# Two-layer hybrid trunk on one core: modulation sums given to other engines, weights' low parts last in a first tile, and GQA's and MLA's transpositions one tile later

## The chip, the cores and the metric

The kernel runs on one core of a Trainium2 chip. The metric is the time of one execution in device microseconds: 1836.56 us before the change, the median of 3 runs (1835.67 to 1840.74).

## The reference: what is computed

Two layers of a hybrid trunk for 9 token tiles of 128 (one of context, eight of latent tokens), model width 1024. Each layer makes a modulation from a condition (two rows: context and latent), normalises, shifts and scales, and then does one wide input projection whose columns go to four head groups:

```python
shift, scale, gate = jnp.split(silu(c) @ w_ada[l] + b_ada[l], 3, axis=-1)
h = rms_norm(x, p['norm_pre']) * (1 + scale) + shift
u = h @ p['w_in']
qa = rms_norm(gq.reshape(B, N, GQA_HEADS, HEAD_DIM), p['gqa_q_norm'])   # GQA: rotated, then attention
cq = rms_norm(mcq, p['mla_q_norm']); ckv = rms_norm(mckv, p['mla_kv_norm'])   # MLA
xbc = jax.nn.silu(centred_dwconv(sxbc, p['ssd_conv_w'], p['ssd_conv_b']))   # SSD
...
o = jnp.concatenate([o_a, o_b, o_c, o_d], axis=-1) @ p['w_out']
y = x + gate * rms_norm(o, p['norm_post'])
```

The change lies in the input projection `h @ w_in` and in the modulation of layer 1, which is computed beside the input projection of layer 0.

## The kernel before

The input projection of a layer is done in pieces of columns, one after the other: LV (512 columns, with GLA's values), SM (296 small columns), MG (gates of MLA), XBC (the columns that SSD's convolution takes), GQA (512), MLA (352), and UQ and QK (MLA's second projection and GLA's q and k). This is called a stage here. Attention, the scans and the output projection follow.

*Products.* Weights and activations are split into a high and a low part, and three products are made per block k of 128 rows (8 blocks): whi·hh, whi·hl and wlo·hh, 24 matmuls per tile. `load_w` brings one block: SP issues the DMA of wst (2 buffers in layer 0, 4 in layer 1), DVE casts it to whi (L257), POOL subtracts to get wlo (L261). `proj_tok` puts tokens on the partitions, and has one PSUM tile per token tile; `proj_T` puts columns on the partitions, and has one PSUM tile of 384 tokens for each of three chunks of every 128 columns (6 in MG, 12 in XBC and in QK). Four PSUM tiles psP go round (`psAB`). A tile is handed to `consume`, which empties it: in GQA (`cons_gqa`) ACT squares it (sq), DVE sums per head (ss, L606), POOL takes the power -0.5 (L107), DVE scales from PSUM (z, L609), POOL and DVE rotate (L611 to L626, r), TensorE transposes r three times (gT, L629) and ACT copies the result. `cons_mla` does the like, with transposes mT (L677).

*Order in a tile before.* `proj_tok` takes, in its first two tiles, all whi·hh and wlo·hh by k and then the eight whi·hl; in the others, and always in `proj_T`, the three products of one k together.

*Modulation.* `ada_steps` is a generator that makes half a part of a modulation (part 1 scale, part 0 shift, part 2 gate; half 0 and 1) in nine steps: for each k it loads 256 KB (ast, 2 buffers) and adds ast times the condition's two rows (r = 0 and 1) into acc; then TensorE sums acc over partitions (ada, L183 for part 2, L189 for the others). For k = 0 ACT writes acc. Else a row's sum is one DVE instruction (L176), or, for r = 1 of part 2, a product on ACT (pr, L173) and a sum on POOL (L174):

```python
elif r and part == 2:
    act.activation(out=pr, in_=st, func=AF.Identity, scale=c)
    pool.tensor_tensor(out=acc[:, r, :], in0=acc[:, r, :], in1=pr, op=ALU.add)
else:
    dve.scalar_tensor_tensor(out=acc[:, r, :], in0=st, scalar=c, ...)
```

`steps_` holds the generators that run in layer 0's projections: part 2 of layer 0 and the six halves of layer 1. `proj_tok` takes two steps after an even tile and one after an odd one, `proj_T` one after each tile.

*What sets the order.* The program is built with a scheduler that simulates it and places each instruction on its engine when it is ready; the program's text only gives the priority. On the chip each engine works through its list in that order, so a waiting instruction holds all behind it on its engine.

Of the kernel before, what the change touches and what calls it, by code (L numbers as in the profile page):

```python
# [12 lines left out]
ALU = mybir.AluOpType  # L13
# [6 lines left out]
KD = 8  # L20
# [14 lines left out]
def hybrid_trunk_kernel(ctx: ExitStack, tc: tile.TileContext, a):  # L35
# [14 lines left out]
    def psC(name="psC"):  # L50
        return ps.tile([128, 512], F32, name=name, tag="C", bufs=1)
# [107 lines left out]
    def ada_steps(l, parts, wpool, ac, sc, d_gate):  # L159

        for part, half in parts:
            o = part * D + half * 512
            acc = wpool.tile([128, 2, 512], F32, name="acc", tag="acc", bufs=1)
            for k in range(KD):
                st = wpool.tile([128, 512], F32, name="ast", tag="ast", bufs=2)
                sp.dma_start(out=st, in_=a["w_ada"][l, k * 128:(k + 1) * 128, o:o + 512])
                for r in range(2):
                    c = cc[:, k, r:r + 1]
                    if k == 0:
                        act.activation(out=acc[:, r, :], in_=st, func=AF.Identity, scale=c)  # L170
                    elif r and part == 2:
                        pr = wpool.tile([128, 512], F32, name="pr", tag="pr", bufs=1)
                        act.activation(out=pr, in_=st, func=AF.Identity, scale=c)  # L173
                        pool.tensor_tensor(out=acc[:, r, :], in0=acc[:, r, :], in1=pr, op=ALU.add)  # L174
                    else:
                        dve.scalar_tensor_tensor(out=acc[:, r, :], in0=st, scalar=c, in1=acc[:, r, :], op0=ALU.mult, op1=ALU.add)  # L176
                yield
            p = psC("ada")
            if part == 2:
# [88 lines left out]

    def proj_tok(l, hh, hl, wpool, off, n, consume, rows=iter(())):
        ws = [load_w(a["w_in"][l, k * 128:(k + 1) * 128, off:off + n], n, wpool) for k in range(KD)]  # L270
        next(rows, None)
        next(rows, None)
        for t in range(T):
            next(rows, None)
            p = psAB()
            s = slice(t * 128, (t + 1) * 128)
            pairs = [(k, x, i) for k in range(KD) for x, i in ((hh, 0), (hh, 1), (hl, 0))]
            if t < 2:
                pairs.sort(key=lambda z: z[1] is hl)
            pairs = [(x[:, k, s], ws[k][i][:, 0:n]) for k, x, i in pairs]  # L280
            mm3(p[:, 0:n], pairs)
            consume(t, p)
            for _ in range(2 - t % 2):
                next(steps_[0], None)

    def proj_T(l, hh, hl, wpool, off, nct, consume, after=None):
        n = nct * 128
        ws = [load_w(a["w_in"][l, k * 128:(k + 1) * 128, off:off + n], n, wpool) for k in range(KD)]
        for ct in range(nct):
            c = slice(ct * 128, (ct + 1) * 128)  # L290
            for ch in range(3):
                s = slice(ch * 384, (ch + 1) * 384)
                p = psAB()
                pairs = []
                for k in range(KD):
                    hi, lo = ws[k]
                    pairs += [(hi[:, c], hh[:, k, s]), (hi[:, c], hl[:, k, s]), (lo[:, c], hh[:, k, s])]
                mm3(p[:, 0:384], pairs)
                consume(ct, ch, p)
                next(steps_[0], None)  # L300
            if after is not None:
                after(ct)
# [76 lines left out]
    for l in range(L):  # L379
# [83 lines left out]
        with st1:  # L463
# [134 lines left out]
            def cons_gqa(t, p):  # L598
# [27 lines left out]
                dve.tensor_tensor(out=r, in0=r, in1=sq, op=ALU.add)  # L626
                tp = psD("gT")
                for i in range(3):
                    pe.transpose(tp[:, i * 128:(i + 1) * 128], r[:, i * 128:(i + 1) * 128], ident)  # L629
                act.copy(qT[:, :, t * 128:(t + 1) * 128], tp[:, 0:256].rearrange("p (a b) -> p a b", b=128))  # L630
                act.copy(kT[:, kt * 128:(kt + 1) * 128], tp[:, 256:384])

            proj_tok(l, hh, hl, wp, G_GQA, 512, cons_gqa)

# [16 lines left out]
            def cons_mla(t, p):  # L651
# [23 lines left out]
                pool.tensor_tensor(out=kr, in0=kr, in1=r[:, 0:32], op=ALU.add)  # L675
                tp = psD("mT")
                pe.transpose(tp[:, 0:128], z[:, 0:128], ident)  # L677
                pe.transpose(tp[0:64, 128:256], z[:, 128:192], ident)
                pe.transpose(tp[:, 256:384], z[:, 192:320], ident)
                s = slice(t * 128, (t + 1) * 128)  # L680
                act.copy(c1h[:, s], tp[:, 0:128])
                dve.tensor_tensor(out=c1l[:, s], in0=tp[:, 0:128], in1=c1h[:, s], op=ALU.subtract)
                act.copy(c2s[0:64, s], tp[0:64, 128:256])
                dve.tensor_tensor(out=c2s[64:128, s], in0=tp[0:64, 128:256], in1=c2s[0:64, s], op=ALU.subtract)
                s = slice(kt * 128, (kt + 1) * 128)
                act.copy(ckh[:, s], tp[:, 256:384])
                dve.tensor_tensor(out=ckl[:, s], in0=tp[:, 256:384], in1=ckh[:, s], op=ALU.subtract)

# [792 lines left out]
```

## Time and profile before

| | before |
|---|---|
| median of 3 runs | 1836.56 us (1835.67 to 1840.74) |
| profiled execution | 1836.28 us, its span 1834.5 us |
| mean granted clock of TensorE | 0.973 |
| busy: PE, DVE, ACT, POOL | 1718.5, 1177.2, 859.9, 729.2 us |
| layer 0, SM to QK | 102.67 to 422.32 us |
| layer 1, SM to QK | 1014.63 to 1296.38 us |

PE is TensorE's matmul, DVE VectorE, ACT ScalarE, POOL GpSimd, SP the queue that issues most DMAs. PEclk is the clock that TensorE was granted, as a share of full speed. Idle time is given with the instruction that ended it.

### The profile page before, as it was taken

The page shows a single profiled execution, that of the slowest core. Times are in us where ns is not written, and L with a number is a line of the kernel's source. Part 1 is how long each engine was busy: PE and PEld are TensorE (multiplying, and loading weights), DVE is VectorE, ACT ScalarE, POOL GpSimd, SP SyncE. Part 2 cuts the span into 40 slices and gives each one's busy share as a digit, 9 for nine tenths or more (in the row PEclk, how much of TensorE's full clock was granted, in tenths as well). Part 3 has the DMA queues.
Part 4 walks back from the last instruction along what each step waited for, and adds up shares of the span by engine and source line. Part 5 has one row for each costly group of instructions (what it writes and reads, how often), then busy time and mean ns, then how long its engine had stood idle before and what let it go on. Part 6 is the DMA issues. An engine that isn't in the chain of part 4 may idle for free.

```text
span 1834.5 us, 25155 instructions
## 1 busy us (share of the span) xinstructions
PE 1718.5 (94%) x8200; PEld 1312.8 (72%) x8200; DVE 1177.2 (64%) x2297; ACT 859.9 (47%) x1907; POOL 729.2 (40%) x909
## 2 busy tenths in 40 slices
PE   8999998998998998999999999999999899899998
PEld 2787977896665666656887999889666666565676
DVE  5738887647877886772453447543776788678223
ACT  4634422434654765673442162132465467567322
POOL 3633149824343543330343323871434354333011
PEclk9999988999989999999999999999998999999999
DMA  8435353413323321142433333231442332114243
GB/s 296 138 117 156 113 168 103 129 63 119 115 77 85 90 79 47 41 144 86 138 129 104 102 94 91 60 102 37 122 116 76 81 88 83 50 36 149 87 137 115
DMA packets 179684, 190.99 MB, mean 104 GB/s; under 512 B 29406, under 2 KB 140720, under 8 KB 179552
## 3 DMA queue, kind: packets, MB, share of 16 engines
q1 hardware_dynamic: 174208, 179.11, 32.1%
q10 hardware_dynamic: 5344, 10.26, 1.7%
q8 instruction: 65, 1.06, 0.3%
q14 instruction: 67, 0.55, 0.1%
HBM read 141.00 MB, written 48.30 MB: 103 GB/s over the span
## 4 chain that ended last, share of the span: by engine, by line
PE 54%; DVE 17%; DMA 11%; POOL 7%; issue 5%; ACT 4%; SPq 1%; ACTq 0%; POOLq 0%; DVEq 0%
PE psP L267 19%; PE op L267 8%; PE st L1102 5%; PE po L1118 5%; DMA ast<-in_w_ada_dram 2%; PE mx L755 2%; DMA wst<-in_w_in_dram 2%; DVE mx L756 2%; DVE Pl L1110 2%; PE po L1114 1%; DVE acc L176 1%; DMA R<-d_rec 1%; POOL wlo L261 1%; DVE d_DT L1023 1%; PE go L931 1%
## 5 line engine op out<-in xcount | busy, mean ns | idle before, releaser
L756 DVE TENSOR_REDUCE mx<-mx 128x1 f32<-128x512 f32 (+2 forms) x400 | 224.6, 582 | 92.2 <-PE mx L755 90.6
L267 PE MATMUL psP<-whi,hh 128*128 128x512 f32 (+2 forms) x576 | 202.6, 363 | 6.1 <-DVE whi L257 3.7
L267 PE MATMUL psP<-wlo,hh 128*128 128x512 f32 (+2 forms) x576 | 202.8, 361 | 2.1 <-POOL wlo L261 1.9
L267 PE MATMUL psP<-whi,hl 128*128 128x512 f32 (+2 forms) x576 | 187.5, 359 | 0.1
L261 POOL TENSOR_TENSOR wlo<-wst,whi 128x512 fp32r<-128x512 f32 (+3 forms) x106 | 130.6, 1240 | 137.9 <-DVE whi L257 79.0
L267 PE MATMUL psP<-hh,whi 128*128 128x384 f32 x480 | 163.1, 340 | 4.7 <-DVE whi L257 3.8
L1102 PE MATMUL st<-QA,KA 128*128 128x512 f32 (+1 forms) x336 | 164.0, 488 | 0.6 <-DVE Pl L1110 0.4
L267 PE MATMUL psP<-hl,whi 128*128 128x384 f32 x480 | 160.2, 336 | 0.0
L267 PE MATMUL psP<-hh,wlo 128*128 128x384 f32 x480 | 155.0, 337 | 0.1
L1110 DVE TENSOR_TENSOR Pl<-st,Ph 128x512 fp32r<-128x512 f32 x160 | 109.7, 686 | 65.9 <-ACT st L1108 64.2
L1107 ACT ACTIVATE Ph<-st 128x512 fp32r<-128x512 f32 x160 | 95.5, 597 | 107.5 <-PE st L1102 99.1
L1117 ACT ACTIVATE P<-st 128x512 f32<-128x512 f32 (+1 forms) x176 | 99.8, 567 | 79.1 <-PE st L1102 67.1
L1102 PE MATMUL st<-QB,KB 66*128 66x512 f32 (+3 forms) x336 | 133.0, 401 | 0.0
L267 PEld LDWEIGHTS psP<-whi,hh 128*128 128x128 f32 x576 | 110.3, 193 | 20.3 <-DVE whi L257 5.2
L267 PEld LDWEIGHTS psP<-wlo,hh 128*128 128x128 f32 x576 | 110.4, 193 | 17.9 <-POOL wlo L261 5.3
L267 PEld LDWEIGHTS psP<-whi,hl 128*128 128x128 f32 x576 | 108.5, 192 | 12.4 <-DVE hl L226 0.3
L1102 PEld LDWEIGHTS st<-QA,KA 128*128 128x128 f32 x336 | 65.4, 195 | 49.8 <-issue 39.3
L267 PEld LDWEIGHTS psP<-hh,whi 128*128 128x128 f32 x480 | 90.1, 188 | 12.0 <-DVE whi L257 5.5
L1102 PE MATMUL st<-QB,KA 96*128 96x512 f32 (+1 forms) x168 | 93.2, 555 | 2.1 <-ACT P L1117 1.8
L1108 ACT ACTIVATE st<-st 128x512 f32<-128x512 f32 x160 | 94.8, 592 | 0.0
L1118 PE MATMUL po<-P,vm 128*65 128x512 f32 (+1 forms) x176 | 88.7, 586 | 5.9 <-ACT P L1117 3.4
L1144 POOL TENSOR_TENSOR gt<-gt,R 128x512 f32<-128x512 f32 (+1 forms) x24 | 26.6, 1106 | 166.0 <-DMA R<-d_rec 162.3
(369 smaller groups left out, 4325.2 us busy)
## 6 DMA issues: line engine op xcount, KB each, us to landing
ast<-in_w_ada_dram SPq DMA_DIRECT2D x96, 256.0 KB
wst<-in_w_in_dram SPq DMA_DIRECT2D x64, 256.0 KB
wost<-in_w_out_dram SPq DMA_DIRECT2D x16, 512.0 KB
d_xs<-d_xb SPq DMA_DIRECT2D x32, 192.0 KB
ot<-d_oT SPq DMA_DIRECT2D x18, 320.0 KB
d_tok<-vv SPq DMA_DIRECT2D x18, 256.0 KB
d_gt<-gg SPq DMA_DIRECT2D x24, 192.0 KB
g_qk<-d_qk SPq DMA_DIRECT2D x36, 128.0 KB
```

The source lines that it names most:

```text
L176: dve.scalar_tensor_tensor(out=acc[:, r, :], in0=st, scalar=c, in1=acc[:, r, :], op0=ALU.mult, op1=ALU.add)
L261: eng.tensor_tensor(out=lo[:, 0:n], in0=st[:, 0:n], in1=hi[:, 0:n], op=ALU.subtract)
L267: pe.matmul(p, lhsT=lt, rhs=rh, start=(first and i == 0), stop=(last and i == n - 1))
L755: pe.matmul(p[:, 0:n], lhsT=lt_m[:, s], rhs=rh_m[:, o:o + n], start=True, stop=True)
L756: dve.tensor_reduce(out=mx[:, t, i:i + 1], in_=p[:, 0:n], axis=AX.X, op=ALU.max)
L1102: anchors["pe"] = pe.matmul(sp_[:, 0:nq], lhsT=kx[:, ks], rhs=qx[:, qs], start=(i == 0), stop=(i == len(spasses) - 1))
L1107: act.activation(out=Ph[:, 0:nq], in_=sp_[:, 0:nq], func=AF.Exp, scale=scale)
L1108: anchors["act"] = act.activation(out=sp_[:, 0:nq], in_=sp_[:, 0:nq], func=AF.Exp, scale=scale)
L1110: anchors["dve"] = dve.tensor_tensor(out=Pl[:, 0:nq], in0=sp_[:, 0:nq], in1=Ph[:, 0:nq], op=ALU.subtract)
L1117: anchors["act"] = act.activation(out=P[:, 0:nq], in_=sp_[:, 0:nq], func=AF.Exp, scale=scale)
L1118: pe.matmul(po[0:65, 0:nq], lhsT=v[:, kt, vi, :], rhs=P[:, 0:nq], start=(j == 0), stop=last, skip_group_check=True)
L1144: pool.tensor_tensor(out=g[:, 0:nq], in0=g[:, 0:nq], in1=R[:, 0:nq], op=ALU.mult)
```

## The change

- `ada_steps`: the row r = 1 goes to ACT and POOL also for part 1 (both halves); for part 2, half 0, of layer 1 only for odd k. There is one more `yield`, ahead of the matmuls, so half a part has ten steps.
- `proj_tok` takes two steps after every tile (GQA one), `proj_T` one (MG two).
- In the first tile of `proj_tok` (LV excepted) and of `proj_T` the order is eight whi·hh, eight whi·hl, eight wlo·hh. The second tile of `proj_tok` keeps its order.
- GQA's and MLA's transposes, and the copies behind them, are returned as a function `rest`, which is called after the next tile has been consumed.

```diff
-                    elif r and part == 2:
+                    elif r and (part != 0 if part < 2 or half else k % 2 or l == 0):
...
                 yield
+            yield
             p = psC("ada")
...
-    def proj_tok(l, hh, hl, wpool, off, n, consume, rows=iter(())):
+    def proj_tok(l, hh, hl, wpool, off, n, consume, rows=iter(()), pace=2):
...
+        rest = None
         for t in range(T):
...
-            if t < 2:
+            if t == 0 and off != G_LV:
+
+                pairs.sort(key=lambda z: (z[2], z[1] is hl))
+            elif t < 2:
                 pairs.sort(key=lambda z: z[1] is hl)
...
-            consume(t, p)
-            for _ in range(2 - t % 2):
+
+            last, rest = rest, consume(t, p)
+            if last is not None:
+                last()
+            for _ in range(pace):
                 next(steps_[0], None)
...
+        if rest is not None:
+            rest()
+
+    def proj_T(l, hh, hl, wpool, off, nct, consume, after=None, pace=1):
...
+                pairs = [(i, x, k) for k in range(KD) for i, x in ((0, hh), (0, hl), (1, hh))]
+                if ct + ch == 0:
+                    pairs.sort(key=lambda z: (z[0], z[1] is hl))
...
-                next(steps_[0], None)
+                for _ in range(pace):
+                    next(steps_[0], None)
...
-            proj_T(l, hh, hl, wp, G_MG, 2, lambda ct, ch, p: gate_out(d_gt[2 + ct], ch, p))
+            proj_T(l, hh, hl, wp, G_MG, 2, lambda ct, ch, p: gate_out(d_gt[2 + ct], ch, p), pace=2)
...
+                def rest():
+                    tp = psD("gT")
...
+                return rest
+
+            proj_tok(l, hh, hl, wp, G_GQA, 512, cons_gqa, pace=1)
```

In `cons_mla` the lines from `tp = psD("mT")` to the last subtraction become a `rest` in the same way. Lines move: L176 stays, L257 becomes L258, L261 L262, L267 L268, L606 L616, L609 L619.

TensorE, end of MG's first tiles in layer 0, where the last of the eight weight blocks comes in. psP_1596 (before) and psP_1614 (after) are the first tile, the other psP the three that are open beside it; whi_1592 and whi_1610 are the last block's high part. Before:

```order
L183 MATMUL ada_1730<-acc_1347,pick_81 2x512
L267 MATMUL psP_1596<-hh_96,whi_1592 128x384
L267 MATMUL psP_1596<-hl_97,whi_1592 128x384
L267 MATMUL psP_1631<-hh_96,whi_1592 128x384
L267 MATMUL psP_1631<-hl_97,whi_1592 128x384
L267 MATMUL psP_1666<-hh_96,whi_1592 128x384
```

After:

```order
L184 MATMUL ada_1643<-acc_1316,pick_81 2x512
L268 MATMUL psP_1614<-hh_96,whi_1610 128x384
L268 MATMUL psP_1614<-hl_97,whi_1568 128x384
L268 MATMUL psP_1614<-hl_97,whi_1574 128x384
L268 MATMUL psP_1614<-hl_97,whi_1580 128x384
L268 MATMUL psP_1614<-hl_97,whi_1586 128x384
L268 MATMUL psP_1614<-hl_97,whi_1592 128x384
L268 MATMUL psP_1614<-hl_97,whi_1598 128x384
L268 MATMUL psP_1614<-hl_97,whi_1604 128x384
L268 MATMUL psP_1614<-hl_97,whi_1610 128x384
L268 MATMUL psP_1614<-hh_96,wlo_1570 128x384
```

Behind the last block the first tile had one product of each kind left; now it has one whi·hh, eight whi·hl and the wlo·hh.

POOL, from MG's end to XBC's start in layer 0. Before:

```order
L174 TENSOR_TENSOR acc<-acc,pr 128x512
L261 TENSOR_TENSOR wlo<-wst,whi 128x256
L174 TENSOR_TENSOR acc<-acc,pr 128x512
L261 TENSOR_TENSOR wlo<-wst,whi 128x512 x8
L561 MEMSET xpad 128x2
```

After:

```order
L174 TENSOR_TENSOR acc<-acc,pr 128x512 x5
L262 TENSOR_TENSOR wlo<-wst,whi 128x512 x2
L174 TENSOR_TENSOR acc<-acc,pr 128x512
L262 TENSOR_TENSOR wlo<-wst,whi 128x512 x2
L174 TENSOR_TENSOR acc<-acc,pr 128x512
L262 TENSOR_TENSOR wlo<-wst,whi 128x512
L174 TENSOR_TENSOR acc<-acc,pr 128x512
L262 TENSOR_TENSOR wlo<-wst,whi 128x512
```

The eight low parts of XBC's weights stood in one piece; modulation sums now stand between them.

DVE, start of GQA in layer 0, from the last casts to the second z. Before:

```order
L257 CAST whi<-wst 128x512
L176 SCALAR_TENSOR_TENSOR acc<-ast,cc,acc 128x512 x2
L257 CAST whi<-wst 128x512
L176 SCALAR_TENSOR_TENSOR acc<-ast,cc,acc 128x512 x10
L606 TENSOR_REDUCE ss_2429<-sq 128x6
L606 TENSOR_REDUCE ss_2487<-sq 128x6
L609 TENSOR_TENSOR z<-psP,ss_2429 128x384
L117 TENSOR_TENSOR sc<-ada,bc 128x8
L176 SCALAR_TENSOR_TENSOR acc<-ast,cc,acc 128x512
L609 TENSOR_TENSOR z<-psP,ss_2487 128x384
```

After:

```order
L258 CAST whi<-wst 128x512
L588 SCALAR_TENSOR_TENSOR yc<-xpad,yc 128x1156
L176 SCALAR_TENSOR_TENSOR acc<-ast,cc,acc 128x512 x7
L616 TENSOR_REDUCE ss_2493<-sq 128x6
L176 SCALAR_TENSOR_TENSOR acc<-ast,cc,acc 128x512
L616 TENSOR_REDUCE ss_2541<-sq 128x6
L176 SCALAR_TENSOR_TENSOR acc<-ast,cc,acc 128x512 x2
L619 TENSOR_TENSOR z<-psP,ss_2493 128x384
L176 SCALAR_TENSOR_TENSOR acc<-ast,cc,acc 128x512 x2
L619 TENSOR_TENSOR z<-psP,ss_2541 128x384
```

Ten sums stand between the last cast and the first z in both; the two reductions (of the first and second tile) have moved in among them.

## Rows read from the trace of the kernel before

**Rows 1.** Windows of layer 0: MG, GQA, MLA, and the sum from SM to QK

```profile
core 0: us, PE busy (x) PEld busy (x) DVE busy (x) ACT busy (x) POOL busy (x), PEclk, DMA share, GB/s
136.12:175.50 39.38, 35.84 (x187) 29.82 (x185) 31.74 (x59) 18.94 (x31) 14.90 (x16) 1.00 0.48 149
...
231.56:297.01 65.45, 61.23 (x278) 50.07 (x277) 55.10 (x70) 13.97 (x34) 40.01 (x37) 0.92 0.47 137
297.01:349.81 52.80, 46.78 (x269) 43.40 (x268) 33.14 (x62) 20.21 (x81) 45.60 (x76) 0.90 0.36 102
...
sum 319.65, PE 302.68 PEld 271.30 DVE 221.51 ACT 115.15 POOL 157.65; mean PE 50.45 PEld 45.22 DVE 36.92 ACT 19.19 POOL 26.27
```

**Rows 2.** Windows of layer 1: the sum over the same six stages

```profile
sum 281.75, PE 276.65 PEld 256.60 DVE 145.21 ACT 87.20 POOL 114.09; mean PE 46.11 PEld 42.77 DVE 24.20 ACT 14.53 POOL 19.02
```

**Rows 3.** Waits of PE in layer 0's stages: us in total, times, longest

```profile
PE gT L629 <- DVE r L626: 4.8, 4, 2.6
PE psP L267 <- DVE whi L257: 4.5, 6, 1.5
PE ada L189 <- DVE acc L176: 3.5, 1, 3.5
```

**Rows 4.** Waits of PE in layer 1's stages

```profile
PE gT L629 <- DVE r L626: 1.1, 1, 1.1
PE mT L677 <- DVE z L660: 1.0, 1, 1.0
...
PE psP L267 <- DVE z L609: 0.9, 2, 0.7
```

**Rows 5.** Windows around TensorE's clock in layer 0 (columns as in rows 1)

```profile
137.30:140.70 3.40, 2.13 (x13) 1.81 (x11) 2.71 (x4) 1.39 (x4) 1.28 (x1) 1.00 0.45 125
256.80:260.20 3.40, 1.16 (x6) 0.62 (x4) 2.40 (x4) 1.08 (x4) 0.00 (x0) 1.00 0.48 151
260.20:270.40 10.20, 8.95 (x29) 7.74 (x30) 7.41 (x11) 1.33 (x2) 7.42 (x9) 0.50 0.34 91
...
301.20:304.60 3.40, 3.40 (x12) 3.40 (x13) 1.69 (x4) 1.33 (x2) 3.40 (x5) 0.50 0.19 53
...
311.40:318.20 6.80, 5.44 (x20) 4.75 (x19) 5.03 (x7) 1.89 (x5) 6.36 (x7) 0.50 0.56 168
```

**Rows 6.** Timeline of PE, MG's start: start us, us, operation [idle before <-releaser]

```profile
140.90 0.44 PE L267 MATMUL psP<-hh,whi 128*128 128x384 f32 x1 [1.47 <-DVE whi L257]
...
143.11 0.33 PE L267 MATMUL psP<-hh,whi 128*128 128x384 f32 x1
143.28 0.33 PE L267 MATMUL psP<-hl,whi 128*128 128x384 f32 x1
143.46 0.33 PE L267 MATMUL psP<-hh,wlo 128*128 128x384 f32 x1
```

**Rows 7.** Groups of layer 0's stages, DVE and POOL: busy us, mean ns | idle before

```profile
L176 DVE SCALAR_TENSOR_TENSOR acc<-ast,cc,acc 128x512 f32<-128x512 f32 x84 | 76.0, 930 | 18.4 <-DMA ast<-in_w_ada_dram 16.1 <-ACT acc L170 1.8
...
L174 POOL TENSOR_TENSOR acc<-acc,pr 128x512 f32<-128x512 f32 x28 | 38.4, 1373 | 18.7 <-ACT pr L173 11.4 <-ACT lgl L479 7.2
```

**Rows 8.** Timeline of DVE: MG's sums, XBC's start, GQA's start

```profile
150.55 0.74 DVE L176 SCALAR_TENSOR_TENSOR acc<-ast,cc,acc 128x512 f32<-128x512 f32 x1
...
180.53 2.27 DVE L176 SCALAR_TENSOR_TENSOR acc<-ast,cc,acc 128x512 f32<-128x512 f32 x2 [0.36 <-DMA ast<-in_w_ada_dram]
...
260.54 1.42 DVE L176 SCALAR_TENSOR_TENSOR acc<-ast,cc,acc 128x512 f32<-128x512 f32 x2 [0.87 <-DMA ast<-in_w_ada_dram]
261.87 1.00 DVE L606 TENSOR_REDUCE ss<-sq 128x6 f32<-128x384 f32 x2
264.24 0.56 DVE L609 TENSOR_TENSOR z<-psP,ss 128x384 f32<-128x384 f32 x1 [1.37 <-POOL ss L107]
```

**Rows 9.** Timeline of POOL, XBC's start

```profile
180.30 1.29 POOL L261 TENSOR_TENSOR wlo<-wst,whi 128x512 fp32r<-128x512 f32 x1 [3.41 <-DVE whi L257]
183.27 1.27 POOL L261 TENSOR_TENSOR wlo<-wst,whi 128x512 fp32r<-128x512 f32 x1 [1.68 <-DVE whi L257]
186.01 1.29 POOL L261 TENSOR_TENSOR wlo<-wst,whi 128x512 fp32r<-128x512 f32 x1 [1.47 <-DVE whi L257]
```

**Rows 10.** Timeline of PE, GQA's start

```profile
261.43 3.72 PE L189 MATMUL ada<-pick,acc 128*128 128x2 f32 x16 [3.47 <-DVE acc L176]
265.01 0.77 PE L267 MATMUL psP<-whi,hh 128*128 128x512 f32 x1
```

More of the change, by code (lines that the diff above doesn't have):

```diff
@@ L281, in proj_tok @@
             mm3(p[:, 0:n], pairs)
-            consume(t, p)
-            for _ in range(2 - t % 2):
+            last, rest = rest, consume(t, p)
+            if last is not None:
+                last()
+            for _ in range(pace):
                 next(steps_[0], None)
-    def proj_T(l, hh, hl, wpool, off, nct, consume, after=None):
+        if rest is not None:
+            rest()
+    def proj_T(l, hh, hl, wpool, off, nct, consume, after=None, pace=1):
         n = nct * 128
@@ L293, in proj_T @@
                 p = psAB()
[L294 to L298, printed above, removed]
+                pairs = [(i, x, k) for k in range(KD) for i, x in ((0, hh), (0, hl), (1, hh))]
+                if ct + ch == 0:
+                    pairs.sort(key=lambda z: (z[0], z[1] is hl))
+                mm3(p[:, 0:384], [(ws[k][i][:, c], x[:, k, s]) for i, x, k in pairs])
                 consume(ct, ch, p)
-                next(steps_[0], None)
+                for _ in range(pace):
+                    next(steps_[0], None)
             if after is not None:
@@ L626, in cons_gqa @@
                 dve.tensor_tensor(out=r, in0=r, in1=sq, op=ALU.add)
[L627 to L633, printed above, removed]
+                def rest():
+                    tp = psD("gT")
+                    for i in range(3):
+                        pe.transpose(tp[:, i * 128:(i + 1) * 128], r[:, i * 128:(i + 1) * 128], ident)
+                    act.copy(qT[:, :, t * 128:(t + 1) * 128], tp[:, 0:256].rearrange("p (a b) -> p a b", b=128))
+                    act.copy(kT[:, kt * 128:(kt + 1) * 128], tp[:, 256:384])
+                return rest
+            proj_tok(l, hh, hl, wp, G_GQA, 512, cons_gqa, pace=1)
             ck = wk.tile([128, 2, 128], F32, name="ck", tag="z", bufs=2)
@@ L675, in cons_mla, with rest @@
                 pool.tensor_tensor(out=kr, in0=kr, in1=r[:, 0:32], op=ALU.add)
[L676 to L687, printed above, removed]
+                def rest():
+                    tp = psD("mT")
+                    pe.transpose(tp[:, 0:128], z[:, 0:128], ident)
+                    pe.transpose(tp[0:64, 128:256], z[:, 128:192], ident)
+                    pe.transpose(tp[:, 256:384], z[:, 192:320], ident)
+                    s = slice(t * 128, (t + 1) * 128)
+                    act.copy(c1h[:, s], tp[:, 0:128])
+                    dve.tensor_tensor(out=c1l[:, s], in0=tp[:, 0:128], in1=c1h[:, s], op=ALU.subtract)
+                    act.copy(c2s[0:64, s], tp[0:64, 128:256])
+                    dve.tensor_tensor(out=c2s[64:128, s], in0=tp[0:64, 128:256], in1=c2s[0:64, s], op=ALU.subtract)
+                    s = slice(kt * 128, (kt + 1) * 128)
+                    act.copy(ckh[:, s], tp[:, 256:384])
+                    dve.tensor_tensor(out=ckl[:, s], in0=tp[:, 256:384], in1=ckh[:, s], op=ALU.subtract)
+                return rest
             proj_tok(l, hh, hl, wp, G_MLA, 352, cons_mla)
```

## The prediction

> **What bounds the kernel now.** I read the views from wide to narrow: windows by stage, waits, clock windows, timelines. The windows by stage come first: in layer 0's projections TensorE is busy 302.68 of 319.65 us [rows 1], in layer 1's 276.65 of 281.75 us [rows 2]. The same matmuls are done in both, but layer 0 also carries the modulation sums of layer 1, and takes 37.9 us more. So what the change can gain in layer 0 is a part of TensorE's idle time, 17.0 us, and of its time at half clock; in layer 1 a part of 5.1 us. Outside these two stages the order of every engine is the old one, so I count nothing there.
>
> The waits of TensorE tell where the idle time is [rows 3]: four waits of a transposition gT for DVE's r (4.8 us), six for a DVE cast of weights (4.5 us) and one for the modulation sum (3.5 us). In layer 1 the largest are 1.1 us for gT, 1.0 us for mT and 0.9 us for z [rows 4]. The clock windows give the rest [rows 5]: the granted clock is 0.50, the lower of the two levels (1.2 GHz against 2.4), from 260.20 to 270.40, from 301.20 to 304.60 and from 311.40 to 318.20 us; ahead of the first of these stretches TensorE was busy 1.16 of 3.40 us. There is no such stretch in layer 1.
>
> What sets the pace at a stage's start is the arrival of weights. Four PSUM tiles are open there, and each new block k gives TensorE three matmuls for each of them. It does these, and then waits for the next cast [rows 6].
>
> **The change part by part.** All terms are in us on TensorE's path; below zero is faster.
>
> *The sums.* 14 of part 1's sums go from DVE to ACT and POOL, and 3 of part 2's go back. DVE loses 11 sums of 930 ns [rows 7], 10.2 us; POOL gains 11 of 1373 ns, 15.1 us, and ACT the products for them. None of the three is TensorE, so this counts only where a cast, a low part or z comes earlier or later; that is priced with the stages below. Costed at nothing by itself: the cover is ACT's and POOL's idle time (POOL works 157.65 of 319.65 us in layer 0 [rows 1]). Where POOL has no idle time, in MLA's start, the order gives it fewer sums than before.
>
> *The yields.* Eight steps more in all, and other steps per tile. The order of DVE up to the start of MG is the old one, so SM costs nothing.
>
> *Low parts last, MG.* The first tile now takes its eight whi·hh products first, and its other 16 only when all eight whi are there. Until the last cast it offers one matmul per k where it offered three, so 7 x 2 = 14 matmuls move behind the last cast. Matmuls of 384 columns follow each other at 0.173 us (143.11, 143.28, 143.46) [rows 6]: 14 x 0.173 = 2.4 us. The casts come no earlier, since the DVE, POOL and SP orders ahead of them are unchanged, and the idle time that the 14 matmuls leave is the same wait grown longer (1.47 us at 140.90 becomes about 2.4). **+2.4**; bounds +1 (some of it filled by small transposes) and +5 (clock, see the rivals).
>
> *Low parts last, XBC.* The same 14 matmuls, +2.4. But here DVE's sums stand in front of the casts: a pair of 2.27 us at 180.53 right before a cast [rows 8]. With one of the two gone the cast comes about 1.1 earlier. POOL now has four sums between its eight low parts; it has idle time there (1.68 us before the one at 183.27, 1.47 before the next [rows 9]) for a sum of 1.37. **+1.3**; bounds -1 (casts gain twice as much) and +4 (POOL's sums hold back the low parts, whose end frees the stage for the next load: two stages only).
>
> *GQA's start.* Here the waits end in the fifth tile: four PSUM tiles are full, and the first is freed only by z, which is at 264.24 behind ten sums, two reductions of sq and a wait for POOL [rows 8]; the 16 modulation matmuls run in its shadow from 261.43 to 265.01, and the first matmul of the fifth tile is at 265.01 [rows 10]. In the new order of DVE the reductions stand among the sums, and z directly behind the tenth, so the 1.37 us for POOL's power falls away and so does most of the two reductions (1.00 us at 261.87). The sums themselves are still ten, paced by loads (0.87 us wait at 260.54). The fifth tile starts about 2.0 earlier. The low parts of the first tile (7 matmuls more behind the last cast) lie in this wait. The modulation matmuls that had run in z's shadow change places with those of the next half part, which ran on the path in MLA: nothing. **-2.0**; bounds -6.5 (with it the half clock: 8.95 us of work in 10.20 at 0.50, half of it 4.5) and +1.6 (7 matmuls of 0.228 with no shadow).
>
> *MLA's start.* POOL is busy 45.60 of 52.80 us there [rows 1]. Between its first and last low part it had three sums, and now two: -1.4, of which I leave 0.4 for one z more (L611) that stands there. The four gT waits (4.8) lie in the same stretch as the waits for weights, so removing one lets the other appear; I take nothing for them. **-1.0**; bounds -4.8 (all gT waits go) and +1.1 (7 matmuls of 352 columns, 0.16 each, held back).
>
> *The transposes one tile later.* They are later in the program's text, but the scheduler places an instruction where it finds it ready. In the new order of layer 0 gT's transposes stand no later among the matmuls than before. In layer 1, with no sums, I take half of the 3.0 us of gT, mT and z [rows 4]: **-1.5**; bounds -3.0 and 0.
>
> Sum: 2.4 + 1.3 - 2.0 - 1.0 - 1.5 = **-0.8 us**. The profiled execution took 1836.28 us (span 1834.5), so 1835.5; the median of the runs stands 0.28 above it, so I forecast 1835.8 us. A measurement here tells about 0.3%, 5.5 us, from no change, and my sum is far inside.
>
> **A rule against the sums' move.** A sum on DVE takes 0.74 us at 150.55, when POOL is idle, and each of the two at 180.53 takes 1.14 beside POOL's low part, so POOL's work is not free for DVE [rows 8]. The Trainium skill, "SBUF — State Buffer", section "Who interferes with whom", says that a DVE instruction with two SBUF inputs contends with a GpSimd instruction that reads SBUF; and "Perfetto Trace Analysis", section "Optimizing Scalar/DVE Operations", that moving work from one to the other might therefore not help. This trace agrees as far as these rows go. Worked out from the rows as a rival below, it would take the XBC and GQA gains away.
>
> **The rivals.**
> (1) *Faster: the idle time before the half clock goes.* If z and the r of GQA come early enough that TensorE is not left idle at 256.80 and in MLA's start, the three stretches at 0.50 run at 1.00. They hold 8.95, 3.40 and 5.44 us of busy time [rows 5], so half of 17.8, 8.9, is gained: -0.8 - 8.9 = -9.7, 1826.9 us. For it: DVE is rid of 10 us, and the sums of the next half part are done sooner. Against: z still has ten sums before it. Chance 0.31.
> (2) *Slower: the held-back matmuls bring the half clock to MG and XBC.* In 137.30 to 140.70 TensorE was busy 2.13 of 3.40 us and kept 1.00; the stretch ahead of 260.20 had 1.16 and got 0.50 [rows 5]. MG's first wait grows by about 0.9 us of matmuls that are held back, and the engine does so much less there. If a stretch such as that from 260.20 follows, that is 10.2 us at half clock, which costs up to 5.1; the same in XBC, whose gain from the casts is then lost too, 5.1 + 1.1. Sum -0.8 + 5.1 + 6.2 = +10.5, 1847.1 us; with MG alone +4.3. It decides in MG's first wait: now 1.47 us with 1.00 granted before and after it, by my count 2.4; the rival holds if 0.50 is granted behind it. Chance 0.18.
> (3) *The sums' move does nothing for DVE.* Each of 11 POOL sums holds a DVE sum for 1.14 - 0.74 = 0.40 us at least, and up to its own 1.37 less what overlaps. Then XBC is +2.4 and GQA 0: -0.8 + 1.1 + 2.0 = +2.3, 1838.9 us. Chance 0.08.
> (4) *The transposes do not change at all* where they wait: without layer 1's 1.5, +0.7, 1837.3 us. Chance 0.08.
>
> **How the numbers follow.** My forecast has 0.35, and (3) and (4), which also lie within 5.5 us, 0.16: together 0.51 for no measurable change. Faster has 0.31 from (1), slower 0.18 from (2). The forecast's own range, from the bounds of its terms (not all at the same end), is 1831 to 1840. For 8 in 10 it must take in most of (1) and of (2): 1826 to 1845.
>
> **What would show it.** In the profile after: the wait for whi in layer 0 grows from 4.5 us to 7 or more, with MG's window about 2.4 longer than 39.38; the fifth GQA tile starts some 2 us after the tenth sum has ended and the one wait of 3.5 for the modulation sum is smaller; gT's 4.8 shrinks while MLA's window loses little. Clock at 0.50 in MG or XBC would prove (2); clock at 1.00 throughout GQA and MLA would prove (1). I am wrong if the casts of MG come at other times, or if layer 1 changes by over 3 us.

## The result and the profile after

The change makes the kernel slower: 1855.16 us (median of 4 runs, 1850.46 to 1855.61) against 1837.62 of the kernel before on the same chip, a ratio of 1.0086 taken over the runs, interval 1.0065 to 1.0107 (the two medians alone would give 1.0095). The forecast was 1835.8 us and no measurable change, range 1826 to 1845. The span of the profiled execution is 1853.0 us, 18.5 more than before: 18.2 more from SM to QK in layer 0, 2.3 more in layer 1's stages, 2.0 less elsewhere.

Windows of the kernel after, in layer 0: MG, XBC, GQA, MLA to UQ's first matmul, and UQ with QK. Columns as in [rows 1].

```profile
136.79:179.14 42.35, 36.00 (x187) 29.76 (x185) 31.41 (x55) 21.98 (x35) 19.36 (x18) 1.00 0.45 138
179.14:246.50 67.36, 61.30 (x347) 59.52 (x348) 49.21 (x54) 33.56 (x56) 27.77 (x31) 0.95 0.43 130
246.50:314.62 68.12, 58.32 (x254) 45.43 (x253) 54.81 (x68) 12.80 (x34) 46.06 (x45) 0.95 0.39 116
314.62:365.07 50.45, 43.92 (x268) 39.37 (x267) 33.34 (x64) 20.68 (x79) 42.91 (x68) 1.00 0.45 132
365.07:440.27 75.20, 72.76 (x389) 64.87 (x389) 33.92 (x70) 20.17 (x52) 21.20 (x30) 1.00 0.23 71
```

Against [rows 1], MG is 2.97 us longer, GQA 2.67, and MLA 2.35 shorter. Two stretches were not in [rows 1]: XBC, and UQ with QK. Kernel before:

```profile
175.50:231.56 56.06, 54.80 (x323) 53.63 (x323) 45.82 (x55) 24.77 (x41) 13.55 (x21) 1.00 0.46 131
349.81:422.32 72.51, 72.29 (x389) 64.78 (x389) 41.67 (x76) 24.90 (x57) 30.02 (x30) 1.00 0.30 94
```

XBC went from 56.06 to 67.36, by 11.3 us, the most by far. Its idle time went from 1.26 to 6.06 (+4.8), 24 more matmuls are done in it, and the mean clock fell to 0.95. The 24 are 16 modulation matmuls more, 9 transposes of XBC's own output (xT) that stood in GQA before, and one small matmul less; they account for about 3 us of the longer busy time, and the lower clock for about 3.4 (see below). POOL is busy 27.77 us there, where it was 13.55. UQ with QK takes 2.7 us more, with the same 389 matmuls, so what MLA gains is lost again behind it.

Layer 1 has no modulation sums beside it. Of its XBC, after and before:

```profile
1093.31:1150.58 57.27, 54.26 (x316) 52.42 (x316) 36.21 (x36) 22.21 (x39) 12.44 (x21) 1.00 0.30 87
```

```profile
1076.57:1130.73 54.16, 53.62 (x316) 52.54 (x316) 36.63 (x36) 22.31 (x39) 13.35 (x22) 1.00 0.32 96
```

The same 316 matmuls take 3.1 us longer. GQA of layer 1 is 0.7 shorter (51.20 against 51.90). The waits of TensorE in layer 0's stages, kernel after (to set beside [rows 3]):

```profile
PE psP L268 <- DVE whi L258: 11.3, 9, 2.5
PE psP L268 <- DVE z L619: 5.7, 2, 5.1
PE psP L268 <- POOL wlo L262: 4.2, 7, 1.6
...
PE ada L190 <- DVE acc L176: 1.6, 1, 1.6
PE ada L190 <- POOL acc L174: 1.4, 1, 1.4
...
PE gT L641 <- DVE r L636: 1.1, 1, 1.1
```

The waits for gT went from 4.8 to 1.1 us, but not through the transposes' later place in the text: without it (e4) they are 1.2. In their place stand 6.8 us more for casts, 3.6 more for low parts, a wait of 5.1 for z in GQA, and waits of the modulation matmuls that now stand in XBC.

What holds up XBC's start can be followed through four engines. Kernel after, the timelines of POOL, ACT and SP, and TensorE:

```profile
190.76 1.29 POOL L262 TENSOR_TENSOR wlo<-wst,whi 128x512 fp32r<-128x512 f32 x1 [1.25 <-DVE whi L258]
194.63 1.26 POOL L174 TENSOR_TENSOR acc<-acc,pr 128x512 f32<-128x512 f32 x1 [2.59 <-ACT pr L173]
195.85 1.26 POOL L262 TENSOR_TENSOR wlo<-wst,whi 128x512 fp32r<-128x512 f32 x1
```

```profile
190.50 1.28 ACT L547 ACT_TABLE_LOAD   x1
...
192.23 1.28 ACT L548 ACT_TABLE_LOAD   x1
...
193.85 0.71 ACT L173 ACTIVATE pr<-ast,cc 128x512 f32<-128x512 f32 x1
```

```profile
194.58 0.33 SPq L166 DMA_DIRECT2D ast<-in_w_ada_dram  x1
195.00 0.38 SPq L256 DMA_DIRECT2D wst<-in_w_in_dram  x1
...
197.15 0.33 SPq L256 DMA_DIRECT2D wst<-in_w_in_dram  x1
```

```profile
195.95 1.72 PE L190 MATMUL ada<-pick,acc 128*128 128x2 f32 x14 [1.44 <-POOL acc L174]
198.80 0.52 PE L268 MATMUL psP<-hh,whi 128*128 128x384 f32 x1 [1.12 <-DVE whi L258]
```

POOL waits 2.59 us for a product that ACT makes only after two table loads of 1.28 us. Behind POOL's sum stands the low part of the sixth block, which so comes at 195.85; its stage is freed at 197.11 and the eighth load goes out at 197.15. In SP's list the seventh load stands behind a modulation load that waits for the same product. TensorE's modulation matmuls wait 1.44 us for the same sum. The eighth and last cast of XBC's weights so starts 20.7 us after the stage's first matmul (at 199.81), where it came 17.1 after it before (192.61 against 175.50).

### The profile page after: what moved, and what is told of

Same layout as the page of the kernel before. It is cut to its first block, busy times and chain, and to the rows that moved or that the text cites. A ratio compares the mean times of both kernels' runs of the same rounds, so it can differ in the third digit from the quotient of the medians.

```text
span 1853.0 us, 25177 instructions
## 1 busy us (share of the span) xinstructions
PE 1720.3 (93%) x8200; PEld 1310.2 (71%) x8200; DVE 1178.3 (64%) x2286; ACT 867.5 (47%) x1918; POOL 744.3 (40%) x920
## 5 line engine op out<-in xcount | busy, mean ns | idle before, releaser
L268 PE MATMUL psP<-whi,hh 128*128 128x512 f32 (+2 forms) x576 | 196.1, 361 | 15.8 <-DVE whi L258 7.1
L268 PE MATMUL psP<-wlo,hh 128*128 128x512 f32 (+2 forms) x576 | 196.9, 359 | 5.9 <-POOL wlo L262 5.4
L268 PE MATMUL psP<-whi,hl 128*128 128x512 f32 (+2 forms) x576 | 187.9, 358 | 0.0
L262 POOL TENSOR_TENSOR wlo<-wst,whi 128x512 fp32r<-128x512 f32 (+3 forms) x106 | 128.9, 1224 | 126.5 <-DVE whi L258 60.3
L268 PE MATMUL psP<-hh,whi 128*128 128x384 f32 x480 | 160.0, 343 | 10.2 <-DVE whi L258 8.3
L268 PE MATMUL psP<-hl,whi 128*128 128x384 f32 x480 | 155.3, 338 | 0.0
L268 PE MATMUL psP<-hh,wlo 128*128 128x384 f32 x480 | 153.0, 338 | 0.3 <-POOL wlo L262 0.3
L268 PEld LDWEIGHTS psP<-whi,hh 128*128 128x128 f32 x576 | 108.4, 191 | 31.5 <-DVE whi L258 9.6
L268 PEld LDWEIGHTS psP<-wlo,hh 128*128 128x128 f32 x576 | 108.2, 191 | 22.6 <-POOL wlo L262 9.5
L268 PEld LDWEIGHTS psP<-whi,hl 128*128 128x128 f32 x576 | 108.4, 192 | 12.1 <-DVE hl L227 0.3
L268 PEld LDWEIGHTS psP<-hh,whi 128*128 128x128 f32 x480 | 90.2, 190 | 16.9 <-DVE whi L258 11.2
L176 DVE SCALAR_TENSOR_TENSOR acc<-ast,cc,acc 128x512 f32<-128x512 f32 x73 | 74.9, 1044 | 32.8 <-DMA ast<-in_w_ada_dram 30.0
```

What stands on the lines that cost most here:

```text
L262: eng.tensor_tensor(out=lo[:, 0:n], in0=st[:, 0:n], in1=hi[:, 0:n], op=ALU.subtract)
L268: pe.matmul(p, lhsT=lt, rhs=rh, start=(first and i == 0), stop=(last and i == n - 1))
```

## The experiments

Each kernel differs from the one before or the one after by the parts named. Stages from first matmul to first matmul in the profiled execution, in us (MLA here with UQ, to QK's first tile); the ratio is to the kernel before on the same chip. Each stage time is of one execution. Three pairs of kernels turn out to have the same order of instructions on every engine, but for a few neighbours that change places (by the names that a trace shows): before and e8, after and e4, e7 and e17. Between the two of a pair the stages of layer 0 differ by up to 1.9 us, XBC of layer 1 by 0.02; a smaller difference in layer 0 says nothing.

| kernel | ratio (95%) | MG 0 | XBC 0 | GQA 0 | MLA 0 | XBC 1 |
|---|---|---|---|---|---|---|
| before | 1 | 39.39 | 56.06 | 65.45 | 68.06 | 54.17 |
| after | 1.0086 (1.0065 to 1.0107) | 42.35 | 67.36 | 68.11 | 70.86 | 57.27 |
| e1: after, old order | 1.0071 (1.0050 to 1.0091) | 39.44 | 67.09 | 66.01 | 72.06 | 54.16 |
| e2: after, old sums | 1.0042 (1.0027 to 1.0058) | 40.99 | 64.69 | 65.09 | 65.90 | 57.27 |
| e3: after, old pace | 1.0097 (1.0067 to 1.0128) | 41.70 | 67.86 | 61.72 | 78.76 | 57.29 |
| e4: after, no deferral | 1.0086 (1.0070 to 1.0101) | 41.24 | 67.98 | 68.18 | 72.78 | 57.29 |
| e5: before + order | 1.0058 (1.0037 to 1.0080) | 40.83 | 61.34 | 62.29 | 71.05 | 57.27 |
| e6: before + sums | 1.0048 (1.0030 to 1.0065) | 39.05 | 65.41 | 63.18 | 75.50 | 54.17 |
| e7: before + pace | 1.0020 (1.0003 to 1.0036) | 39.69 | 61.36 | 67.35 | 67.63 | 54.16 |
| e8: before + deferral | 0.9997 (0.9981 to 1.0013) | 39.18 | 55.42 | 65.59 | 69.30 | 54.19 |
| e9: before + order in proj_T | 1.0055 (1.0035 to 1.0076) | 40.63 | 61.02 | 62.76 | 68.83 | 57.26 |
| e11: e6, DVE adds | 1.0061 (1.0036 to 1.0085) | 38.21 | 57.38 | 68.52 | 78.91 | 54.18 |
| e12: e6, 3 ast buffers | 1.0066 (1.0043 to 1.0089) | 42.16 | 64.55 | 63.15 | 75.00 | 54.16 |
| e14: before, 3 ast buffers | 1.0037 (1.0018 to 1.0056) | 38.46 | 54.57 | 64.37 | 80.71 | 54.16 |
| e15: before, lo last only | 1.0033 (1.0019 to 1.0047) | 40.25 | 60.27 | 64.67 | 67.68 | 55.09 |
| e16: before, two tiles | 1.0101 (1.0079 to 1.0122) | 43.92 | 65.34 | 62.06 | 68.70 | 57.27 |
| e17: after, old order and sums | 1.0043 (1.0027 to 1.0060) | 38.49 | 60.20 | 65.66 | 67.58 | 54.16 |

**One part undone at a time (e1 to e4).** The edits are the lines of the diff above, turned back:

```diff
e1
-            if t == 0 and off != G_LV:
-
-                pairs.sort(key=lambda z: (z[2], z[1] is hl))
-            elif t < 2:
+            if t < 2:
...
-                if ct + ch == 0:
-                    pairs.sort(key=lambda z: (z[0], z[1] is hl))
e2
-                    elif r and (part != 0 if part < 2 or half else k % 2 or l == 0):
+                    elif r and part == 2:
e3
-            yield
...
-            for _ in range(pace):
+            for _ in range(2 - t % 2):
...
-                for _ in range(pace):
+                for _ in range(1):
e4
-            last, rest = rest, consume(t, p)
+            last = consume(t, p)
```

> The changed kernel with the products of a first tile in their old order; sums, pace and transposes stay changed. Order theory (the matmuls held back behind the last weight block cost the time): MG of layer 0 falls from 42.35 back to about 39.4 us, XBC of layer 1 from 57.27 to about 54.2, XBC of layer 0 from 67.36 by most of its 11; total 1855 - 15 = about 1840. Sums theory (a modulation sum on POOL waits for its product on ACT and its load, and holds POOL's low parts, SP's weight loads and TensorE's modulation matmuls behind it, in XBC of layer 0): only the 3 + 3 us of MG and layer 1 come back, XBC of layer 0 stays above 64; total about 1849.

> The changed kernel with the old division of the sums (part 1 wholly on DVE, all of part 2's second row on ACT and POOL); order, pace and transposes stay changed. Sums theory: XBC of layer 0 falls from 67.36 to about 58 to 60 us (before 56.06, plus 2.4 for the held-back matmuls), GQA's wait for z of 5.1 us shrinks; total about 1843 to 1846. Order theory: XBC of layer 0 stays above 64; total above 1851.

> The changed kernel with the old number of modulation steps per tile and nine steps per half part. Pace theory (taking two steps after each tile of MG moves the end of the first half part and its 16 modulation matmuls into XBC's start): XBC of layer 0 falls by 5 us or more and its two waits for the modulation sum (1.6 and 1.4 us) go; total about 1847 to 1850. Sums or order theory: XBC of layer 0 keeps over 64 us; total within 3 us of 1855.

> The changed kernel with GQA's and MLA's transposes called at once again. All three theories: XBC of layer 0 stays at 67.4 us and the total within 3 us of 1855, since the deferral acts only in GQA and MLA. A deferral theory (copies that come later hold up z and the next tile) would give GQA and MLA of layer 0 3 us or more back: 1852 or less.

With the old order, MG and XBC of layer 1 are back at 39.44 and 54.16, but XBC of layer 0 stays at 67.09, as the sums theory has it there, and the total (1.0071) is not clear of 1.0086. With the old sums XBC of layer 0 falls by only 2.7, to 64.69, and the total to 1.0042. So neither theory alone holds, and what is lost in XBC is not a sum of parts: with one cause gone the weights are still late. The last cast starts 21.3 us into XBC in e1 and 19.7 in e2, against 20.7 in the kernel after and 17.1 before. The pace undone leaves XBC where it is and only moves time from GQA to MLA. The deferral undone changes nothing, as e4 has the order of the kernel after.

**One part alone on the kernel before (e5 to e8).**

> The kernel before with only the new order of a first tile's products. Order theory: about 10 to 15 us slower than before (1848 to 1852), XBC of layer 0 above 62 us. Sums theory: only the held-back matmuls, 2.4 to 3 us in each of MG and XBC of layer 0 and XBC of layer 1, so 1842 to 1846.

> The kernel before with only the new division of the sums. Sums theory: 7 to 12 us slower than before (1844 to 1850), with XBC of layer 0 at 62 us or more and a wait for a modulation sum there. Order theory: within 3 us of before, XBC of layer 0 at 56 to 58 us.

> The kernel before with only the new numbers of modulation steps per tile and the added step. Pace theory: 5 us or more slower, the modulation matmuls at XBC's start. Sums or order theory: within 3 us of before.

> The kernel before with only the transposes of GQA and MLA called one tile later. All theories: within 3 us of before; the four waits of gT for r (4.8 us in layer 0) get smaller, and what they hid, waits for weights, takes their place.

Order and sums each cost about half a per cent alone (1.0058 and 1.0048), the pace 1.0020, the deferral nothing. Their plain sum, 1.23%, lies above the 0.86% of all four, but the intervals are too wide to call that a difference. XBC of layer 0 gets 5.3 us longer with the order, 9.4 with the sums and 5.3 with the pace. With the pace TensorE does 32 modulation matmuls in XBC where it did 16, busy 3.7 us for 2.1, and 9 transposes xT more; it is idle 2.3 us there (1.3 before), and the last cast starts 19.8 us into the stage. How the 5.3 us divide between these is not shown. GQA's wait for z grows with the pace too (its idle time from 4.2 to 9.3 us).

The deferral costs nothing because it does nothing: the scheduler placed the transposes where they had been, and e8 has the order of the kernel before. The waits for gT that were expected to shrink in e8 did not. Waits of TensorE in layer 0's stages, e8, then e4:

```profile
PE gT L635 <- DVE r L630: 4.7, 4, 2.6
```

```profile
PE gT L641 <- DVE r L636: 1.2, 1, 1.2
```

**Where in the order (e9), and how much (e15, e16).** All on the kernel before; e9 is e5 with proj_tok as it was, and

```diff
e15
-                    pairs.sort(key=lambda z: (z[0], z[1] is hl))
+                    pairs.sort(key=lambda z: z[0])
e16
-                if ct + ch == 0:
+                if ct == 0 and ch < 2:
```

> The kernel before with the new order of products in proj_T's first tiles alone (MG, XBC, QK). Held-back theory: MG of layer 0 about 41 us, XBC of layer 0 about 58.5 to 61, XBC of layer 1 57.3, together 7 to 10 us slower than before (with the new order everywhere: 0.58%). If the first tiles of proj_tok were to blame instead: within 3 us of before, XBC of layer 1 apart.

> The kernel before, with proj_T's first tile in the order whi.hh and whi.hl by k and then the eight wlo.hh, so that 7 matmuls instead of 14 are held back behind the last weight block. Held-back theory: half of the loss, XBC of layer 1 at 54.17 + 1.5 = about 55.7 us (57.26 with 14 held back), MG of layer 0 at about 40 us, total about 0.25 to 0.35% slower than before. If the change of order as such did it: XBC of layer 1 at about 57.3 us again, or at 54.2.

> The kernel before, with the new order in proj_T's first two tiles, so that 28 matmuls are held back. Held-back theory: about twice the loss, XBC of layer 1 at about 60 us, MG of layer 0 at 42 to 43 us, total 0.9 to 1.2% slower than before. If only the first tile mattered: XBC of layer 1 at about 57.3 us.

proj_T's first tile alone costs as much (1.0055) as the order everywhere. In total the loss grows with the matmuls held back: 0.33% with 7, 0.55% with 14 (these two intervals overlap), 1.01% with 28. By stages it is less even. MG takes 40.25, 40.63 and 43.92 us, and with 28 the half clock comes into MG and XBC, where e9 and e15 have none. MG and XBC of e16:

```profile
138.31:182.22 43.91, 37.06 (x187) 31.07 (x186) 30.65 (x57) 20.91 (x33) 14.03 (x15) 0.96 0.40 127
182.22:247.57 65.35, 59.02 (x336) 57.34 (x336) 50.64 (x59) 24.45 (x42) 13.43 (x22) 0.95 0.44 132
```

Of the 7.6 us that these two stages take more than in e9, the lower clock (3.4 us long in MG, 6.8 in XBC) may explain up to 5.1, an estimate at half of its length. XBC of layer 1 is the cleanest place, since it comes out within 0.05 us of the same in all kernels with the same order of products. Windows of that stage, e15 and e16:

```profile
1079.09:1134.19 55.10, 53.40 (x317) 52.66 (x316) 35.58 (x35) 22.33 (x39) 13.80 (x22) 1.00 0.31 93
```

```profile
1088.58:1145.85 57.27, 54.16 (x316) 52.42 (x316) 36.11 (x36) 22.51 (x39) 13.02 (x21) 1.00 0.29 87
```

+0.9 with 7, +3.1 with 14, and no more with 28: there the expectation of twice the loss missed. XBC of layer 0 already has 4.2 of its 5.0 us with 7 held back. So the amount is not all: with a new order of TensorE's products the scheduler also placed DVE's and SP's work anew. In XBC of layer 1 of the kernel after it can be seen; timeline of DVE:

```profile
1091.17 0.41 DVE L258 CAST whi<-wst 128x512 fp32r<-128x512 f32 x1
1094.73 0.55 DVE L557 SCALAR_TENSOR_TENSOR gg<-gg,psP 128x384 f32<-128x384 f32 x1 [3.15 <-ACT gg L556]
1095.20 0.68 DVE L549 TENSOR_TENSOR lx<-lx,le 128x512 f32<-128x512 f32 x1
1095.81 2.19 DVE L258 CAST whi<-wst 128x512 fp32r<-128x512 f32 x3
```

Three casts stand behind MG's last gates, for which DVE waits 3.15 us. The last cast ends 11.6 us after the stage's first matmul (at 1104.87), where it ended 10.0 after it (1086.57 against 1076.57); in e15 it ends 9.1 after it (1088.17), so the +0.9 there came with earlier weights. Of the +3.1, the later cast can be 1.6; the rest is not divided further.

**What of the sums holds XBC up (e11, e12, e14).** All with the old order; e11 and e12 on e6, e14 on the kernel before:

```diff
e11
-                        pool.tensor_tensor(out=acc[:, r, :], in0=acc[:, r, :], in1=pr, op=ALU.add)
+                        (pool if part == 2 else dve).tensor_tensor(out=acc[:, r, :], in0=acc[:, r, :], in1=pr, op=ALU.add)
e12, e14
-                st = wpool.tile([128, 512], F32, name="ast", tag="ast", bufs=2)
+                st = wpool.tile([128, 512], F32, name="ast", tag="ast", bufs=3)
```

> The kernel before with the new division of the sums, but with part 1's products from ACT added by DVE instead of POOL. POOL theory (POOL's sums hold back the low parts): XBC of layer 0 falls from 65.4 to 60 us or less. ACT theory (the product stands in ACT's list behind table loads of 1.28 us and behind DVE's lx, so that the load's buffer is held, and SP's list, in order, cannot issue the next weight load behind the next modulation load): XBC of layer 0 stays at 63 us or more.

> The kernel before with the new division of the sums and with three buffers instead of two for the modulation loads, so that SP's list is not held by a buffer that ACT has not yet read. ACT theory: XBC of layer 0 falls from 65.4 to 58 to 61 us, and no modulation load waits 2 us or more in SP's list between weight loads there. POOL theory: XBC stays at 63 us or more.

> The kernel before with three buffers for the modulation loads alone: what the third buffer does by itself. All theories: within 4 us of before, XBC of layer 0 at 54 to 58 us.

With a third buffer XBC stays at 64.55 us, which by the expectation speaks against the ACT theory, that the product's lateness does its harm through SP's list; the trace, below, is less plain. With part 1's additions taken off POOL it is back at 57.38, though ACT's products still stand among its table loads. XBC in e6 and in e11:

```profile
174.54:239.95 65.41, 60.20 (x336) 58.14 (x336) 47.58 (x47) 34.58 (x57) 32.00 (x33) 0.95 0.44 132
```

```profile
174.82:232.20 57.38, 55.72 (x325) 53.96 (x326) 47.92 (x58) 34.12 (x55) 15.29 (x22) 1.00 0.44 129
```

POOL is busy 15.29 us there in place of 32.00, TensorE's idle time is 1.66 in place of 5.21, and the clock stays at 1.00. The last cast of XBC's weights, in the kernel before, e6, e11 and e12 (the stage's first matmul is at 175.50, 174.54, 174.82 and 178.01):

```profile
192.61 0.43 DVE L257 CAST whi<-wst 128x512 fp32r<-128x512 f32 x1 [1.52 <-DMA wst<-in_w_in_dram]
```

```profile
198.45 0.41 DVE L257 CAST whi<-wst 128x512 fp32r<-128x512 f32 x1
```

```profile
192.11 1.24 DVE L257 CAST whi<-wst 128x512 fp32r<-128x512 f32 x1 [0.47 <-DMA wst<-in_w_in_dram]
```

```profile
196.88 1.43 DVE L257 CAST whi<-wst 128x512 fp32r<-128x512 f32 x1 [0.35 <-DMA wst<-in_w_in_dram]
```

It starts 17.1 us into the stage before, 23.9 in e6, 17.3 in e11 and 18.9 in e12. So part 1's additions on POOL make XBC's weights late, and with them gone the weights come as before. By which way is not shown to the end: POOL's sums stand before the low parts, but in e11 modulation loads also wait less for ACT's product in SP's list (3.3 us between XBC's start and 200 us, 6.4 in e6). The third buffer brought the last cast 5 us nearer too, so the way through SP's list has a part; XBC of e12 gained only 0.9 by it, since TensorE waits there 3.6 us for DVE's convolution (xT for yc), where it does so for 0.2 in e6. The scheduler also placed loads and sums anew, and what of the 8.0 us is due to that is not shown apart.

The total of e11 is no better (1.0061), because GQA and MLA take more. The third buffer alone has XBC 1.5 us shorter and MLA 12.7 longer, and is 0.37% slower, where at most 4 us were expected. In all kernels with the new sums, and in e14, all modulation work has ended by QK, and 28 sums fall into MLA and UQ where 21 do before; these stages take 70.9 to 80.7 us there and 65.9 to 71.1 in the others. Whether the one causes the other was not tried apart.

**Both causes away (e17).** e1 and e2 together.

> The changed kernel with the old order of products and the old division of the sums; pace, added step and deferral stay changed. If order and sums are the causes: no more than the pace alone, 0.0 to 0.3% slower than before, XBC of layer 1 at 54.2 us, XBC of layer 0 at about 61 us with 32 modulation matmuls in it. If something in the deferral costs: 0.4% or more.

Of 0.86%, 0.43% remains (0.27 to 0.60): more than expected. It is not the deferral: e17 has the order of e7, the pace alone, which measured 0.20 (0.03 to 0.36); the two intervals overlap and measure one thing. So order and sums make up half or more of the loss in the kernel after, and the pace the rest, with XBC at 60.20 us and none of the long waits.

No version here beats the kernel before; the nearest is the deferral alone, which is the same.

## Why the prediction was wrong

**MG: right within what can be told.** +2.4 was forecast; it is +3.0 in the kernel after, +1.9 in e4, which has the same order, and +1.2 in e9. The first wait there became 2.55 us for 1.47 [rows 6], with 2.4 forecast. Timeline of TensorE after:

```profile
141.96 0.62 PE L268 MATMUL psP<-hh,whi 128*128 128x384 f32 x2 [2.55 <-DVE whi L258]
```

The clock stayed at 1.00, so rival (2) did not come in MG; with twice as many matmuls held back (e16) it did.

**XBC: the step that failed.** "POOL now has four sums between its eight low parts; it has idle time there (1.68 us [...]) for a sum of 1.37", priced at +1.3 and at most +4; it was +11.3. (In the trace after, three sums stand between them.) POOL's idle time in [rows 9] was time in which it waited for a cast. A sum in front of a low part has its own wait, for ACT's product, up to 2.59 us, and the low part waits with it; with two stages only, the load two blocks later waits too. I counted durations against idle time, and not what a waiting sum holds behind it. In e11 8.0 us of XBC's time went with part 1's additions on POOL.

**The yields and steps: "SM costs nothing" and no term at all for XBC.** The order showed the modulation matmuls; I did not look where the first half part's 16 would fall. With two steps after each tile of MG they fall in XBC's start, 32 in place of 16. In e7, where this is all that changed, XBC takes 5.3 us more, 1.6 of it the matmuls themselves.

**The half clock.** In XBC it came twice, after idle time. Windows of the kernel after:

```profile
183.70:185.10 1.40, 0.22 (x2) 0.22 (x2) 1.40 (x2) 1.37 (x3) 0.58 (x1) 1.00 0.89 245
185.20:188.60 3.40, 3.40 (x12) 3.39 (x12) 1.84 (x3) 3.37 (x5) 2.89 (x3) 0.52 0.45 140
195.95:198.80 2.85, 1.73 (x15) 1.64 (x15) 0.48 (x2) 1.42 (x3) 1.28 (x4) 1.00 0.83 249
198.80:202.20 3.40, 3.40 (x11) 3.40 (x12) 1.49 (x4) 0.53 (x1) 2.91 (x5) 0.53 0.40 115
```

That is 6.8 us at the lower level, which cost about half, 3.4 by estimate. Rival (2) had the half clock in XBC, for a wait of another kind (the held-back matmuls).

**GQA: -2.0 forecast, +2.7 measured.** The mechanism behind z holds: its chain has no wait for POOL's power any more (z follows its sums at once, at 281.74). But the last cast, which started 18.8 us after the stage's first matmul before (at 250.40), came 22.4 after it (at 268.90), because the sums of the new order stand between the casts. The pace put them there: in e3, without it, the last cast starts 16.2 us into the stage and GQA takes 61.72 us; in e7, with it alone, 23.0 and 67.35. Timeline of DVE after:

```profile
250.43 0.43 DVE L258 CAST whi<-wst 128x512 fp32r<-128x512 f32 x1
...
251.56 2.44 DVE L176 SCALAR_TENSOR_TENSOR acc<-ast,cc,acc 128x512 f32<-128x512 f32 x2
253.93 1.41 DVE L585 SCALAR_TENSOR_TENSOR yc<-xpad,cw,yc 128x1156 f32<-128x1156 f32 x1
255.26 0.41 DVE L258 CAST whi<-wst 128x512 fp32r<-128x512 f32 x1
...
268.90 0.43 DVE L258 CAST whi<-wst 128x512 fp32r<-128x512 f32 x1
...
281.74 0.55 DVE L619 TENSOR_TENSOR z<-psP,ss 128x384 f32<-128x384 f32 x1
```

The step that failed took the weights' times as given and moved only z.

**MLA: -1.0 forecast, -2.35 measured** to UQ's first matmul, and the clock there is 1.00 where it was 0.90, one half of rival (1). The sum had no term for UQ and QK behind it, which take 2.7 more: TensorE is idle 2.4 us there, where it was 0.2. The sign was right by luck: the term was for idle time, which grew there from 6.0 to 6.5 us, and the gain is in busy time, 43.92 for 46.78 us, beside the higher clock. From MLA's start to QK's end nothing of it is left: 125.65 us for 125.31.

**Layer 1: -1.5 forecast, +2.3 measured** from SM to QK: XBC +3.1, GQA -0.7. The -1.5 was for the transposes one tile later, and rival (4), with 0.08, is what came: they did not move (e8, e4). And I had priced the held-back matmuls in layer 0's stages alone, though the order of products changes in layer 1 as well; [rows 4] shows no wait for weights there (the trace has one, of 0.4 us, in XBC), and I read that as a margin.

**The sums' gain for DVE: forecast 10.2 us, measured 1.1.** Groups of DVE and POOL in layer 0's stages, kernel after:

```profile
L176 DVE SCALAR_TENSOR_TENSOR acc<-ast,cc,acc 128x512 f32<-128x512 f32 x73 | 74.9, 1044 | 32.8 <-DMA ast<-in_w_ada_dram 30.0 <-ACT acc L170 2.0 <-DVE acc L176 0.3
```

```profile
L174 POOL TENSOR_TENSOR acc<-acc,pr 128x512 f32<-128x512 f32 x39 | 56.2, 1441 | 45.5 <-ACT pr L173 30.5 <-ACT lgl L489 7.0 <-ACT acc L170 6.1
```

DVE has 11 sums fewer, but the other 73 take 1044 ns each in place of 930 [rows 7], so it is busy with them 74.9 us in place of 76.0. This was rival (3), which had 0.08. Its least price per sum, 0.40 us, was about half of what came (9.1 us for 11 sums, 0.83 each), as 1.14 was the mean of the pair at 180.53, not each of the two: one takes 1.61 us, beside POOL's low part, and the other 0.74, behind it. The pair in the kernel before (least, median and longest in ns):

```profile
L176 DVE SCALAR_TENSOR_TENSOR acc<-ast,cc,acc x2: 739/1174/1609, 180.5 to 182.1; 128x512 f32<-128x512 f32 x2
```

I also gave the rival only the lost gains and not the loss in XBC. The Trainium skill, "SBUF — State Buffer", section "Who interferes with whom", says that a DVE instruction with two SBUF inputs contends with a GpSimd instruction that reads SBUF; these rows agree with it.

The slower side, rival (2), thus had the right sign, but most of the loss came by a mechanism that I had not priced, and its 0.18 was too little.

## What to carry to other kernels

Before work is moved to an engine with idle time, ask what each moved instruction will wait for, and what stands behind it in that engine's list: a sum of 1.3 us that waited 2.6 for its input held up a low part, a buffer and the next load. Where matmuls are fed by weights as they come, an order that leaves fewer of them ready per block was paid at the end here, also in a stage that hardly waited for weights before. Before a gain is booked for moving a piece in the program's text, see in the new order whether it moves at all: the deferred transposes did not. And when a schedule is made by a program, see where every moved piece lands on the bound engine (here 16 modulation matmuls in XBC), since a cause taken away alone may leave the time where it is.

## What was not expected of the hardware

Additions given to POOL bought DVE nothing here. In e6 and e11 DVE does the same 73 sums, and 14 additions are done by POOL in e6 and by DVE in e11. Groups of DVE in layer 0's stages, e6, then e11:

```profile
L176 DVE SCALAR_TENSOR_TENSOR acc<-ast,cc,acc 128x512 f32<-128x512 f32 x73 | 75.2, 1049 | 26.3 <-DMA ast<-in_w_ada_dram 23.9 <-ACT acc L170 2.2
```

```profile
L176 DVE SCALAR_TENSOR_TENSOR acc<-ast,cc,acc 128x512 f32<-128x512 f32 x73 | 64.0, 894 | 24.8 <-DMA ast<-in_w_ada_dram 23.6 <-ACT acc L170 1.0
...
L174 DVE TENSOR_TENSOR acc<-acc,pr 128x512 f32<-128x512 f32 x14 | 11.4, 816 | 0.0
```

DVE is busy 75.2 us in the one and 64.0 + 11.4 = 75.4 in the other: 14 additions on POOL made DVE's own sums longer by 11.2 us, 0.80 each, as much as it needs to do the 14 itself.
